# Up-projection by block products: seven products of a pair in another order, and a statistics matmul issued later

## The chip, the cores and the metric

The kernel runs on one core of a Trainium2 chip. The metric is device time in microseconds (us) of one execution, the median of several runs. TensorE (PE) does the matmuls and loads their weights (PEld), VectorE (DVE), ScalarE (ACT) and GpSimd (POOL) the elementwise work, and SyncE (SP) issues the DMAs.

## What is computed

One layer of a hybrid encoder trunk on 512 tokens of width 2048, in float32. The change concerns the feed-forward part alone:

```
h  = h + W_down( relu( RMSNorm(h) W_up )^2 )        W_up: 2048 x 8192, W_down: 8192 x 2048
y  = RMSNorm_final(h)
RMSNorm(x) = x * rsqrt(mean(x*x) + 1e-6) * w
```

Ahead of it stand an input projection, neighbourhood attention, a bidirectional gated delta rule and the output projection, none of which is edited.

## The kernel before

**Operands.** Every float32 matmul operand is split into a high part (a rounding cast on ACT, line 94) and the rest (a subtraction on DVE, line 95); a product is three matmuls, high times high, high times low and low times high (lines 907 to 909). Activations stay transposed: features on partitions, tokens on the free axis.

**Up-projection.** The 8192 output features are taken as 32 pairs of two 128-wide tiles. For one pair, weights and activations are seen as 2 x 2 blocks: A11, A12, A21, A22 are [128, 1024] weight tiles (1024 input features by 128 outputs), and the activations are halved by features and by tokens (lo_t, hi_t, 256 tokens each). As in Strassen's scheme seven products instead of eight are made, each with a sum of weight blocks (S1 = A21 + A22, S2 = S1 + A11, S4 = S2 + A12, S3 = A21 + A11) and a sum of activation blocks (T1 to T4, made once). A product is 8 blocks of 3 matmuls of 256 columns, 24 matmuls. S1, S2 and S4 are made one after the other in place, in the tile of A22 (`p.a22`, later `p.s2`), by adds on DVE (line 914); S3 is made in the tile of A21.

**Banks.** A pair has three PSUM banks, a, b and c (`BANK`, line 920). P6 and P7 add onto what is in bank b (P1, then P1 + P6), P3 onto bank c (P5); Q4, P1, P5 and P2 start a bank anew (`FIRST`). Between two products of one bank, the partial sum is taken out: ACT copies Q4 (line 980), P5 (982), P1 (984) and P6 (986) from PSUM into the halves of two [128, 2, 256] tiles, tA and tB; DVE adds these to the later sums (lines 988 to 995). A matmul into a bank waits for the copy out of it. Then follow a maximum or minimum with zero times the norm's factor (DVE, lines 990 and 999), a square (ACT) and a store to DRAM (SP, lines 1002 and 1003).

**Order.** `ORDER` (line 922) gives the products of a pair: Q4, P5, P1, P6, P7, P3, P2. Pairs 0 and 1 are done together, product by product (line 1050), with P1 and P2 of both made earlier (lines 1013 to 1017); pairs 2 to 29 one at a time; pairs 30 and 31 together (line 1053). The queues of the engines are not filled strictly in the order of the code: at compile time a planner takes, for each engine, the first instruction in code order that its own costs say is ready. In the trace P3 is thus cut in two, with P7 between its parts. On the chip each queue runs in the order so fixed.

**Buffers.** High and low weight parts have three buffers each (line 898), raw weight tiles four, A21/A22 seven (line 1025), tA/tB four (line 1028), and the output tiles r0, r1 share four with the later reloads of hidden tiles (`ev`, line 78).

**Start of the stage.** The last output tiles of the output projection give the sums of squares for the norm (`sumsq`, line 820). `stat` (line 829) is a task that is advanced once every 12 up-projection matmuls (`pump`): at its first step it makes eight matmuls with one column (lines 833 and 834), then DVE's twelve small steps for the reciprocal root and a diagonal tile (lines 142 to 146); three steps later comes the matmul that broadcasts the factor (line 149). Meanwhile ACT and DVE split the activation operands (line 862). The tiles of pairs 0 and 1 lie in memory that the unsplit T1 to T4 (`TR`) held before. After pair 31 the first 16 hidden tiles are reloaded (line 1054) and the down-projection begins.

Of the kernel before, what the change touches and what calls it, by code (L numbers as in the profile page):

```python
# [10 lines left out]
F32 = mybir.dt.float32  # L11
# [8 lines left out]
T = 512  # L20
# [29 lines left out]
def tile_hybrid_block(  # L50
# [5 lines left out]
    V, S_, PE, G = nc.vector, nc.scalar, nc.tensor, nc.gpsimd  # L56
# [20 lines left out]
    def ev(name):  # L77
        return st.tile([128, T], F32, tag="ev", name=name, bufs=4)
# [19 lines left out]
    tasks = []  # L98
# [31 lines left out]
    def rsqrt(pool, a, n, nm):  # L130
        y = pool.tile([128, n], F32, tag="rsy", name=f"rsy_{nm}", bufs=2)
        u = pool.tile([128, n], F32, tag="rsu", name=f"rsu_{nm}", bufs=2)
        return newton_rsqrt(y, u, a)
# [5 lines left out]
    def rstd_bcast(ps, sumsq, nm, cs=range(4), wait=0, dg=None):  # L139
        n, lo = len(cs), cs[0]  # L140
        a = cp.tile([128, 4], F32, tag="rsa", name=f"rsa_{nm}", bufs=2)
        V.tensor_scalar(out=a[:, :n], in0=sumsq[:, lo : lo + n], scalar1=1.0 / D, scalar2=EPS, op0=ALU.mult, op1=ALU.add)
        rs = rsqrt(cp, a[:, :n], n, nm)
        dg = ev(f"dg_{nm}") if dg is None else dg
        V.tensor_tensor(out=dg[:, : n * 128].rearrange("p (c i) -> p c i", c=n), in0=ident[:, None, :].to_broadcast([128, n, 128]),
                        in1=rs[:, :, None].to_broadcast([128, n, 128]), op=ALU.mult)
        for _ in range(wait):
            yield
        PE.matmul(ps[:, lo * 128 : (lo + n) * 128], ones, dg[:, : n * 128], start=True, stop=True)
# [32 lines left out]
    with ExitStack() as p0:  # L182
# [27 lines left out]
        def mtile(key, view=None):  # L210
            ps = mm()
            for u in range(2):
                unit_mm(ps, fetch(key, u), X, 8 * u, u == 0, u == 1, view)
            return ps
# [96 lines left out]
        for r in (127, 0):  # L311
            t = dn.tile([128, 128], F32, name=f"sel{r}")
# [411 lines left out]
        i = 3  # L724
# [40 lines left out]
        for h in range(NH):  # L765
            qkv = []
            for e, kind in enumerate(("aq", "ak", "av")):
                ps = mtile((kind, h), perm)
                t = ap.tile([128, T], F32, tag=kind, name=f"{kind}{h}", bufs=1 if e < 2 else 2)
# [5 lines left out]
            t = att_task(h, *qkv, ap)  # L775
# [8 lines left out]
    with ExitStack() as p1:  # L784
# [3 lines left out]
        def bank():  # L788
            return mmp.tile([128, T], F32, tag="mm", name="ps_b")
# [27 lines left out]
        tp = p1.enter_context(tc.tile_pool(name="tp", bufs=1, side="right", reuse_waits="tile"))  # L817
        acc = tp.tile([128, T], F32, name="sacc")

        def sumsq(src, m, nm, ts=slice(0, T)):  # L820
            sq = tp.tile([128, T], F32, tag="sq", name=f"sq{nm}", bufs=2)
            S_.activation(out=sq[:, ts], in_=src[:, ts], func=AF.Square)
            if m == 0:
                V.tensor_copy(out=acc, in_=sq)
            elif m < 15:
                V.tensor_tensor(out=acc[:, ts], in0=acc[:, ts], in1=sq[:, ts], op=ALU.add)
            return sq

        def stat(nm, sq, cs=range(4)):
            ps = sxp.tile([128, T], F32, tag="sx", name="ps_s")  # L830
            for c in cs:
                b = slice(c * 128, (c + 1) * 128)
                PE.matmul(ps[:, c : c + 1], acc[:, b], ones[:, 0:1], start=True, stop=False)
                PE.matmul(ps[:, c : c + 1], sq[:, b], ones[:, 0:1], start=False, stop=True)
            ps2 = bank()
            yield from rstd_bcast(ps2, ps, nm, cs, 3)
            ts = slice(cs[0] * 128, (cs[-1] + 1) * 128)
            S_.copy(out=rB[:, ts], in_=ps2[:, ts])
            return ps2
# [8 lines left out]
        lo_t, hi_t = slice(0, 256), slice(256, 512)  # L848
# [15 lines left out]
        with ExitStack() as p5:  # L864
# [3 lines left out]
            for n, m in enumerate(m for j in range(8) for m in (j, j + 8)):  # L868
                ps = bank()
# [6 lines left out]
                sq = sumsq(xr, n, f"h{m}")  # L876
# [20 lines left out]
            def wsplit(raw, name):  # L897
                hi = st.tile([128, 1024], F32R, tag="wh", name=f"wh_{name}", bufs=3)
                lo = st.tile([128, 1024], F32R, tag="wl", name=f"wl_{name}", bufs=3)
                return split(raw, hi, lo)  # L900
# [12 lines left out]
            def add(out, x, y, op=ALU.add):  # L913
                V.tensor_tensor(out=out, in0=x, in1=y, op=op)  # L914
# [4 lines left out]
            ROLE = {"P1": "11", "P2": "21", "P3": "22", "Q4": "T4", "P5": "T1", "P6": "T2", "P7": "T3"}  # L919
            BANK = {"P1": "b", "P6": "b", "P7": "b", "P5": "c", "P3": "c", "Q4": "a", "P2": "a"}  # L920
            FIRST = {"P1", "P5", "Q4", "P2"}
            ORDER = ("Q4", "P5", "P1", "P6", "P7", "P3", "P2")

            def open_pair(nm, a11, a12):
                p = Pair()
# [38 lines left out]
            def up_m(i):  # L964
                m0 = i // 8 * 16 + i % 8
                return m0, m0 + 8

            def up_open(i):
                m0, m1 = up_m(i)
                return open_pair(f"u{i}", load_raw(wup[m0, 0], f"A11_u{i}"), load_raw(wup[m0, 1], f"A12_u{i}"))  # L970

            def up_evac(i, p, q, et):
                ps = p.ps[BANK[q]]
                if not hasattr(p, "tA"):
                    p.tA, p.tB = et(f"tA_u{i}"), et(f"tB_u{i}")
                    p.r0, p.r1 = ev(f"r0_u{i}"), ev(f"r1_u{i}")
                    p.left = 7
                tA, tB, r0, r1 = p.tA, p.tB, p.r0, p.r1
                if q == "Q4":
                    S_.copy(out=tA[:, 0], in_=ps)  # L980
                elif q == "P5":
                    S_.copy(out=tB[:, 0], in_=ps)
                elif q == "P1":
                    S_.copy(out=tA[:, 1], in_=ps)  # L984
                elif q == "P6":
                    S_.copy(out=tB[:, 1], in_=ps)
                elif q == "P7":
                    add(r1[:, hi_t], ps, tB[:, 0])
                    add(r1[:, lo_t], ps, tA[:, 0])
                    V.scalar_tensor_tensor(out=r1, in0=r1, scalar=0.0, in1=rB, op0=ALU.min, op1=ALU.mult)  # L990
                    S_.activation(out=r1, in_=r1, func=AF.Square)
                elif q == "P3":
                    add(r0[:, hi_t], ps, tB[:, 1])
                else:
                    add(r0[:, lo_t], ps, tA[:, 1])
                p.left -= 1
                if p.left:
                    return
                V.scalar_tensor_tensor(out=r0, in0=r0, scalar=0.0, in1=rB, op0=ALU.max, op1=ALU.mult)
                S_.activation(out=r0, in_=r0, func=AF.Square)  # L1000
                m0, m1 = up_m(i)
                nc.sync.dma_start(out=hidD[m0], in_=r0)
                nc.sync.dma_start(out=hidD[m1], in_=r1)
# [3 lines left out]
            for i, p in enumerate(first):  # L1007
                for q in ("P1", "P2"):
                    heads[i, q] = wsplit(p.a11 if q == "P1" else p.a12, f"{q}_u{i}") if (i, q) in ((0, "P1"), (0, "P2"), (1, "P1")) else None
            tasks.append(stat("h", sq))  # L1010
            for o, j in early_fill[:8]:
                fill(o, j, tr_src[o, j])
            for i, p in enumerate(first):
# [7 lines left out]
        with ExitStack() as p6:  # L1021
            sm = p6.enter_context(tc.tile_pool(name="sm", bufs=1, side="right", reuse_waits="tile"))

            def a_tile(name):
                return sm.tile([128, 1024], F32, tag="a", name=name, bufs=7)

            def et(name):
                return sm.tile([128, 2, 256], F32, tag="et", name=name, bufs=4)

            def more(p, s22, s21):  # L1030
                p.a22, p.a21 = a_tile(f"A22_{p.nm}"), a_tile(f"A21_{p.nm}")
                nc.sync.dma_start(out=p.a22, in_=s22)
                nc.sync.dma_start(out=p.a21, in_=s21)

            def up_group(idx, order, ps=None):
                ps = ps or [up_open(i) for i in idx]
                for i, p in zip(idx, ps):
                    m0, m1 = up_m(i)
                    more(p, wup[m1, 1], wup[m1, 0])
                if order[0] == "P1":  # L1040
                    for q in ("P1", "P2"):
                        for i, p in zip(idx, ps):
                            up_evac(i, p, q, et)
                    order = order[2:]
                for q in order:
                    for i, p in zip(idx, ps):
                        run_product(p, q, a_tile)
                        up_evac(i, p, q, et)

            up_group((0, 1), ("P1", "P2", "Q4", "P5", "P6", "P7", "P3"), first)  # L1050
            for i in range(2, 30):
                up_group((i,), ORDER)
            up_group((30, 31), ORDER)
            hid0 = [load_hid(k) for k in range(16)]
        p7.close()

# [6 lines left out]
        for b in range(NB):  # L1063
# [4 lines left out]
            for m in range(14 if last else 16):  # L1068
                ps = bank()
# [27 lines left out]
        for half in range(2):  # L1097
            ts = slice(half * 256, half * 256 + 256)
            for m in (14, 15):
                ps = bank()[:, 0:256]  # L1100
# [10 lines left out]
                sq = sumsq(H[m], m, f"f{m}_{half}", ts)  # L1111
# [88 lines left out]
```

## Time and profile before

| | before |
|---|---|
| median of 3 runs (lowest, highest) | 2942.87 us (2940.63, 2944.16) |
| the profiled execution's own time | 2942.32 us |
| its span in the trace | 2940.5 us |
| weight loads busy | 2471.8 us (84%) |
| DVE busy | 1687.3 us (57%) |
| ACT busy | 1032.7 us (35%) |
| POOL busy | 24.7 us (1%) |
| granted TensorE clock, mean | 0.995 |

The profile shows one execution. Busy time is the time in which an engine had an instruction under way; a matmul's end is modelled, and matmuls overlap, so the step from one start to the next tells PE's pace. A wait names the instruction whose end released the waiting one.

### The profile page before, as it was taken

What the parts mean: (1) busy time and instruction counts of PE and PEld (TensorE: products, weight loads), DVE (VectorE), ACT (ScalarE), POOL (GpSimd) and SP (SyncE); (2) the same over time, 40 slices, a digit from 0 to 9 for tenths busy, and PEclk for the clock granted to TensorE, in tenths of its full rate; (3) what the DMA queues carried; (4) which work ended last, traced back from release to release, by engine and by line L of the source; (5) the groups of instructions that cost most, each with busy time, mean ns of one, the idle gap of its engine ahead of it and who ended that gap; (6) DMA issues with size and microseconds to landing.
All of it is one profiled execution on the core that took longest, in us unless ns stands there. A gap on an engine that the chain in (4) does not pass through costs nothing.

```text
span 2940.5 us, 39399 instructions
## 1 busy us (share of the span) xinstructions
PE 2872.9 (98%) x15736; PEld 2471.8 (84%) x15736; DVE 1687.3 (57%) x2495; ACT 1032.7 (35%) x1613; POOL 24.7 (1%) x66
## 2 busy tenths in 40 slices
PE   8999999999999999999999999999999999999998
PEld 6778788888788888888879999999997888888887
DVE  6888779744554444444458777777775242332334
ACT  6444322233233333223345444444444232221322
POOL 0000000000000000000000000000000000000000
PEclk9999999999999999999999999999999999999999
DMA  7555663655632323543434333333428242343332
GB/s 231 191 176 187 212 184 120 213 159 166 187 116 94 95 87 119 170 156 111 145 109 165 126 125 127 119 130 122 129 73 271 94 157 94 114 137 100 108 101 86
DMA packets 170872, 412.30 MB, mean 140 GB/s; under 512 B 34368, under 2 KB 46720, under 8 KB 170688
## 3 DMA queue, kind: packets, MB, share of 16 engines
q1 hardware_dynamic: 170016, 407.69, 43.1%
q0 software_dynamic: 672, 2.10, 0.3%
q8 instruction: 123, 2.02, 0.3%
q14 instruction: 61, 0.50, 0.1%
HBM read 350.84 MB, written 58.88 MB: 139 GB/s over the span
## 4 chain that ended last, share of the span: by engine, by line
PE 88%; DVE 5%; DMA 5%; ACT 1%; issue 1%; SPq 0%; DVEq 0%; ACTq 0%
PE ps_b L115 12%; PE ps_b L116 12%; PE ps_b L117 12%; PE ps_mm L115 9%; PE ps_mm L117 9%; PE ps_mm L116 9%; PE ps_b L907 8%; PE ps_b L909 7%; PE ps_b L908 7%; DVE wl_in L90 1%; DMA bB<-rowD 1%; DMA Nd<-bB 1%; DMA gB<-rowD 1%; DMA kb<-rowD 1%; PE ps_ax L589 0%
## 5 line engine op out<-in xcount | busy, mean ns | idle before, releaser
L115 PE MATMUL ps_mm<-xh,wh_in 128*128 128x512 f32 x1416 | 567.1, 400 | 2.8 <-ACT wh_in L89 2.8
L117 PE MATMUL ps_mm<-xh,wl_in 128*128 128x512 f32 x1416 | 560.1, 396 | 0.5 <-DVE wl_in L90 0.5
L116 PE MATMUL ps_mm<-xl,wh_in 128*128 128x512 f32 x1416 | 559.8, 395 | 0.0
L115 PE MATMUL ps_b<-hih,wh_dn 128*128 128x512 f32 x992 | 386.4, 390 | 2.3 <-ACT hih L94 2.3
L117 PE MATMUL ps_b<-hih,wl_dn 128*128 128x512 f32 x992 | 386.5, 390 | 0.3 <-DVE wl_dn L90 0.3
L116 PE MATMUL ps_b<-hil,wh_dn 128*128 128x512 f32 x992 | 386.5, 390 | 0.2 <-DVE hil L95 0.2
L89 ACT CAST wh_in<-raw_in 128x1024 fp32r<-128x1024 f32 x177 | 186.0, 1051 | 414.6 <-PE ps_mm L116 336.4
L117 PEld LDWEIGHTS ps_mm<-xh,wl_in 128*128 128x128 f32 x1416 | 267.6, 189 | 60.7 <-DVE wl_in L90 1.0
L115 PEld LDWEIGHTS ps_mm<-xh,wh_in 128*128 128x128 f32 x1416 | 267.8, 189 | 58.0 <-ACT wh_in L89 3.2
L116 PEld LDWEIGHTS ps_mm<-xl,wh_in 128*128 128x128 f32 x1416 | 268.0, 189 | 55.1 <-issue 0.2
L89 ACT CAST wh_dn<-raw_dn 128x1024 fp32r<-128x1024 f32 x124 | 130.8, 1055 | 460.4 <-PE ps_b L116 451.0
L90 DVE TENSOR_TENSOR wl_dn<-raw_dn,wh_dn 128x1024 fp32r<-128x1024 f32 x124 | 151.9, 1225 | 232.9 <-ACT wh_dn L89 232.8
L90 DVE TENSOR_TENSOR wl_in<-raw_in,wh_in 128x1024 fp32r<-128x1024 f32 x177 | 216.2, 1222 | 120.2 <-ACT wh_in L89 113.7
L907 PE MATMUL ps_b<-XT_x,wh_S_u 128*128 128x256 f32 x768 | 222.9, 290 | 13.0 <-ACT tA_u L984 12.9
L115 PEld LDWEIGHTS ps_b<-hih,wh_dn 128*128 128x128 f32 x992 | 186.4, 188 | 42.4 <-ACT hih L94 3.9
L116 PEld LDWEIGHTS ps_b<-hil,wh_dn 128*128 128x128 f32 x992 | 186.7, 188 | 40.4 <-DVE hil L95 1.7
L117 PEld LDWEIGHTS ps_b<-hih,wl_dn 128*128 128x128 f32 x992 | 186.7, 188 | 39.2 <-DVE wl_dn L90 0.7
L909 PE MATMUL ps_b<-XT_x,wl_S_u 128*128 128x256 f32 x768 | 217.4, 283 | 0.0
L908 PE MATMUL ps_b<-XT_x,wh_S_u 128*128 128x256 f32 x768 | 217.2, 283 | 0.0
L95 DVE TENSOR_TENSOR wl_S_u<-A_u,wh_S_u 128x1024 fp32r<-128x1024 f32 x128 | 156.2, 1223 | 71.8 <-ACT wh_S_u L94 71.6
L94 ACT CAST wh_S_u<-A_u 128x1024 fp32r<-128x1024 f32 x128 | 134.3, 1049 | 144.8 <-DVE A_u L914 129.6
L907 PEld LDWEIGHTS ps_b<-XT_x,wh_S_u 128*128 128x128 f32 x768 | 147.1, 192 | 23.6 <-ACT tA_u L984 18.7
(354 smaller groups left out, 5101.4 us busy)
## 6 DMA issues: line engine op xcount, KB each, us to landing
raw_in<-in_win SPq DMA_DIRECT2D x177, 512.0 KB
raw_dn<-in_wdn SPq DMA_DIRECT2D x124, 512.0 KB
raw_A_u<-in_wup SPq DMA_DIRECT2D x64, 512.0 KB
A_u<-in_wup SPq DMA_DIRECT2D x64, 512.0 KB
raw_wo<-in_wout SPq DMA_DIRECT2D x32, 512.0 KB
hidD<-r_u SPq DMA_DIRECT2D x64, 256.0 KB
hr<-hidD SPq DMA_DIRECT2D x64, 256.0 KB
gD<-g SPq DMA_DIRECT2D x32, 256.0 KB
```

The source lines that it names most:

```text
L89: S_.copy(out=hi, in_=raw)
L90: V.tensor_tensor(out=lo, in0=raw, in1=hi.bitcast(F32), op=ALU.subtract)
L94: S_.copy(out=hi, in_=src)
L95: V.tensor_tensor(out=lo, in0=src, in1=hi.bitcast(F32), op=ALU.subtract)
L115: PE.matmul(ps, hi[:, w], rh, start=first and kk == 0, stop=False)
L116: PE.matmul(ps, hi[:, w], rl, start=False, stop=False)
L117: PE.matmul(ps, lo[:, w], rh, start=False, stop=last and kk == 7)
L907: PE.matmul(ps, hi[:, c], t[:, lo_t], start=first and j == 0, stop=False, skip_group_check=True)
L908: PE.matmul(ps, hi[:, c], t[:, hi_t], start=False, stop=False, skip_group_check=True)
L909: PE.matmul(ps, lo[:, c], t[:, lo_t], start=False, stop=j == 7, skip_group_check=True)
```

## The change

The products of a pair run in the order Q4, P1, P5, P6, P3, P7, P2, and no two that follow each other write one bank. The copies are regrouped, so that tA holds Q4 and P5, and tB P1 and P6; P7's two adds become one over [128, 2, 256] with its sum read twice. There are six tA/tB buffers instead of four, and one for the squares instead of two. Pairs 30 and 31 are done one after the other. For the norm ahead of the up-projection, the task `stat` lets two steps pass before its matmuls and seven instead of three before the broadcast; for the final norm it stays as it was.

```
         def sumsq(src, m, nm, ts=slice(0, T)):
-            sq = tp.tile([128, T], F32, tag="sq", name=f"sq{nm}", bufs=2)
+            sq = tp.tile([128, T], F32, tag="sq", name=f"sq{nm}", bufs=1)
...
-        def stat(nm, sq, cs=range(4)):
+        def stat(nm, sq, cs=range(4), wait=3, lead=0):
+            for _ in range(lead):
+                yield
             ps = sxp.tile([128, T], F32, tag="sx", name="ps_s")
...
-            yield from rstd_bcast(ps2, ps, nm, cs, 3)
+            yield from rstd_bcast(ps2, ps, nm, cs, wait)
...
-            ORDER = ("Q4", "P5", "P1", "P6", "P7", "P3", "P2")
+            ORDER = ("Q4", "P1", "P5", "P6", "P3", "P7", "P2")
...
                 elif q == "P5":
+                    S_.copy(out=tA[:, 1], in_=ps)
+                elif q == "P1":
                     S_.copy(out=tB[:, 0], in_=ps)
-                elif q == "P1":
-                    S_.copy(out=tA[:, 1], in_=ps)
...
                 elif q == "P7":
-                    add(r1[:, hi_t], ps, tB[:, 0])
-                    add(r1[:, lo_t], ps, tA[:, 0])
+                    add(r1.rearrange("p (o t) -> p o t", o=2), ps[:, None, :].to_broadcast([128, 2, 256]), tA)
...
                 else:
-                    add(r0[:, lo_t], ps, tA[:, 1])
+                    add(r0[:, lo_t], ps, tB[:, 0])
...
-            tasks.append(stat("h", sq))
+            tasks.append(stat("h", sq, wait=7, lead=2))
...
             def et(name):
-                return sm.tile([128, 2, 256], F32, tag="et", name=name, bufs=4)
+                return sm.tile([128, 2, 256], F32, tag="et", name=name, bufs=6)
...
-            for i in range(2, 30):
+            for i in range(2, 32):
                 up_group((i,), ORDER)
-            up_group((30, 31), ORDER)
```

## Rows read from the trace of the kernel before

**Rows 1.** The page, busy time and share of the span of each engine.
```profile
PE 2872.9 (98%) x15736; PEld 2471.8 (84%) x15736; DVE 1687.3 (57%) x2495; ACT 1032.7 (35%) x1613; POOL 24.7 (1%) x66
```

**Rows 2.** Stages: length, busy time (instructions) of PE, PEld, DVE, ACT, POOL, PEclk, DMA.
```profile
1530.50:1552.30 21.80, 16.30 (x116) 14.63 (x115) 18.91 (x56) 15.86 (x42) 0.00 (x0) 0.92 0.27 88
...
1583.00:2177.80 594.80, 581.39 (x4706) 567.93 (x4705) 437.59 (x477) 269.31 (x365) 0.00 (x0) 1.00 0.37 122
2177.80:2218.00 40.20, 40.20 (x338) 40.20 (x337) 31.63 (x35) 19.95 (x28) 0.00 (x0) 1.00 0.30 97
2218.00:2245.00 27.00, 24.19 (x92) 17.23 (x91) 14.82 (x22) 12.80 (x20) 0.00 (x0) 0.94 0.87 287
```

**Rows 3.** Waits from 1583 to 2177 us: who for whom, us, times, longest.
```profile
PEld ps_b L907 <- ACT tA_u L984: 18.7, 28, 0.7
...
PE ps_b L907 <- ACT tA_u L984: 12.9, 28, 0.5
PEld ps_b L907 <- ACT tB_u L986: 4.9, 28, 0.2
PEld ps_b L909 <- DVE wl_S_u L95: 3.3, 14, 0.2
```

**Rows 4.** Timeline of one pair, 1803.7 to 1809.6: start, us, instruction, idle before.
```profile
1803.92 0.28 PE L909 MATMUL ps_b<-X_x,wl_A_u 128*128 128x256 f32 x1
...
1804.24 0.37 ACT L984 COPY tA_u<-ps_b 128x256 f32<-128x256 f32 x1 [1.25 <-PE ps_b L909]
...
1804.66 0.39 PE L907 MATMUL ps_b<-XT_x,wh_S_u 128*128 128x256 f32 x1 [0.46 <-ACT tA_u L984]
1804.88 0.28 PE L908 MATMUL ps_b<-XT_x,wh_S_u 128*128 128x256 f32 x1
...
1808.72 0.36 ACT L986 COPY tB_u<-ps_b 128x256 f32<-128x256 f32 x1
...
1808.88 0.28 PE L908 MATMUL ps_b<-X_x,wh_S_u 128*128 128x256 f32 x1
1809.13 0.39 PE L907 MATMUL ps_b<-XT_x,wh_S_u 128*128 128x256 f32 x1
```

**Rows 5.** Groups by line and shape: busy us, mean ns, idle before.
```profile
L95 DVE TENSOR_TENSOR wl_S_u<-A_u,wh_S_u 128x1024 fp32r<-128x1024 f32 x128 | 156.2, 1223 | 71.8 <-ACT wh_S_u L94 71.6
L94 ACT CAST wh_S_u<-A_u 128x1024 fp32r<-128x1024 f32 x128 | 134.3, 1049 | 144.8 <-DVE A_u L914 129.6 <-PE ps_b L908 12.0 <-issue 3.2
L914 DVE TENSOR_TENSOR A_u<-A_u,raw_A_u 128x1024 f32<-128x1024 f32 x96 | 116.8, 1220 | 1.0
L1072 DVE TENSOR_TENSOR Ha<-ps_b,Ha 128x512 f32<-128x512 f32 x62 | 42.9, 692 | 187.6 <-PE ps_b L117 187.6
```

**Rows 6.** The chain that ended last, 1532 to 1558: start, us, what.
```profile
1532.62 0.22 PE ps_s L833 x2
...
1535.29 1.06 ACT wh_P_u L94
...
1548.18 2.44 DVE XT_x L95 x7
...
1550.65 0.65 ACT tA_u L984 x2
...
1552.27 1.24 DVE wl_A_u L95
```

**Rows 7.** Timeline, 1533 to 1544: the root's first and last steps, the broadcast.
```profile
1533.99 0.16 DVE L142 TENSOR_SCALAR rsa_h<-ps_s 128x4 f32<-128x4 f32 x1 [1.15 <-PE ps_s L834]
...
1536.18 0.16 DVE L127 SCALAR_TENSOR_TENSOR rsy_h<-rsu_h,rsy_h 128x4 f32<-128x4 f32 x1
...
1542.62 2.08 PE L149 MATMUL ps_b<-dg_h,ones 128*128 128x512 f32 x2 [4.13 <-DVE dg_h L145]
```

**Rows 8.** The chain that ended last, 2205 to 2226: start, us, what.
```profile
2218.85 4.01 DMA hr<-hidD
...
2223.55 0.74 PE ps_b L115 x2
```

## The prediction

> **What bounds the kernel now.** The page first: TensorE (PE) is busy 98% of the 2940.5 us span [rows 1], so time can only come off where PE is slowed or kept waiting. The table by stage shows where that is. The up-projection's single pairs, from the first product of pair 2 to the first of pair 30, take 594.8 us for 28 pairs of 168 matmuls (4704; the row counts 4706, as two belong to the edges): 21.24 us a pair, 126.4 ns a matmul. The last two pairs, whose products alternate, take 40.2 us for 336: 20.1 us a pair, 119.6 ns a matmul. The granted clock is 1.00 (2.4 GHz) in both, and the matmuls are alike [rows 2]. So a pair run alone costs 1.14 us more than the same work with two pairs interleaved.
>
> The view of waits for this stretch says why: PE and its weight load wait 28 times, once a pair, for the ACT copy of L984 (P1's copy), and the weight load 28 times for that of L986 (P6's copy) [rows 3]. One pair in the timeline shows both. P1's last matmul starts at 1803.92; its copy runs 1804.24 to 1804.61; P6, which adds into the same bank, starts at 1804.66, and its second matmul at 1804.88. Two steps that at 0.12 us each take 0.24 us took 0.96: 0.72 us lost. P6's copy starts only at 1808.72, and P7, again the same bank, at 1809.13, 0.25 us after the last matmul of P3 that the planner had put in between; some 0.25 us is lost there [rows 4]. That makes 0.97 of the 1.14; the rest is the split-up P3, half of whose weights come late in every second pair (the weight load's 14 waits) [rows 3].
>
> How much is there to win? By PE's busy time the stage has 13.4 us of idle, by the weight load's busy time 26.9, by the spacing 594.8 - 28 x 20.1 = 32.0 [rows 2]. The Trainium skill (Perfetto Trace Analysis, section Identifying the Most-Contended Engine) calls matmul busy time a poor measure, since matmuls are pipelined, and prefers the weight load's share: by it the gain would be about 27 us. The trace agrees with the order of the two; I take the spacing, because a delayed pair of matmuls also counts longer (0.39 us at 1804.66 [rows 4]).
>
> **The change, part by part.** *New order Q4, P1, P5, P6, P3, P7, P2.* Between P1 and P6 now lies P5 (bank c), between P6 and P7 lies P3, between P5 and P3 lies P6: each copy has a whole product, 24 x 0.1196 = 2.87 us. The copy needs 0.37 us and started 0.32 us after the last matmul where ACT was free [rows 4]; behind one 1.05 us cast [rows 5] it ends after some 1.7 us. Both waits go. What is late next? The weights: S1, S2 and S4 are made in place in one tile, and P5, P6, P3 now follow each other. Take Q4's start as 0. S1's cast needs a weight buffer (three rotate) that the previous pair's P2 frees at 0; with 1.05 for a cast, 1.22 for a subtraction or an add [rows 5]: S1 ready at 2.3 (wanted at 5.7), S2 added, cast and subtracted by 5.8 (wanted at 8.6), S4 by 9.3 (wanted at 11.5). Slack 2.2 us at the tightest. DVE is busy 437.59 of 594.8 us [rows 2], so one foreign 1.22 us step per link is fine, two are just over. I take no new stall: 28 x 1.14 = **-32.0 us**. Ends: all of it, or up to half kept (below).
>
> *One evacuation add of 512 elements for two of 256, tA/tB regrouped:* 0.69 us (same size out of PSUM) to 1.22 us (1024 elements) [rows 5]; by size the first. The next product writes another bank, so only the squaring behind it waits: 0. Its store goes out one product later in the pair, and what SP has queued behind it with it; those loads are for later pairs: 0. *Six tA/tB buffers:* no wait for them in the pairs' view [rows 3]: 0. *One squares buffer:* each square now waits for the previous add into the running sum, one output tile ago: 0; uncovered, one add, 0.69 us.
>
> *Last two pairs one after the other:* alternating they ran without stall; in the new order also: 0. But pair 30 now ends 20 us before pair 31, so its two output buffers are free for the first reloads of the hidden tiles. Now the third reload leaves at 2218.85 and PE has the tile 4.7 us later [rows 8]; the stretch has 27 us with clock 0.94 [rows 2]. The slot it takes is freed by the split of the first, and with that tile already there the split can follow P2's first blocks, by an estimate up to half a product (1.4 us) sooner: **-1.0**. Ends: -3 (PE's idle 27.0 - 24.2 us [rows 2]) and +2 (pair 31's own stores now both come last).
>
> *Statistics matmuls two steps later, broadcast seven steps after instead of three.* PE visibly stands 4.13 us before the broadcast, as the diagonal tile comes late from DVE [rows 7]. But the chain that ended last does not pass there: it goes from P1's end (cast at 1535.29) over DVE's splits of the transformed operands to 1550.62, ACT's copies, and the split of A22 at 1552.27 [rows 6]. PE would wait there instead, so the visible stall is worth 0. The eight statistics matmuls, on the chain at 0.22 us each, leave it: up to 1.8 us; in return DVE's twelve small root steps, from 1533.99 to 1536.34, now done in idle time (2.4 us), may fall into its busy run [rows 6, 7]. The larger tA/tB pool moves those tiles, whose copies wait for the operands' last reader at 1550.65 [rows 6]. Net **-0.5**; ends -4.1 (the whole stall) and +2.1 (both broadcast passes, 2.08 us, on PE's path [rows 7]).
>
> Sum: -32.0 - 1.0 - 0.5 = -33.5. I keep back 1.5 us for pairs at the edges (pair 2 follows the group in the old order): -32. The profiled execution took 2942.32 us (1.8 around the span), 0.55 below the median of 2942.87. 2942.3 - 32 = 2910.3; on the median's scale **2911 us**.
>
> **The rivals.** *A quarter to half of the stall stays:* DVE runs two foreign steps inside the chain S1, S2, S4, so P3 starts late by 2.44 - 2.2 = 0.24 us, or three, 1.46 us, in some pairs. At 0.24 to 0.5 us a pair 7 to 14 us are given back: 2918 to 2925. For it: three dependent products in a row, DVE at 74%. Against: the operations of P3 are issued ahead of those of P7.
>
> *Slower:* S3's subtraction stands before S4's add in DVE's queue. It waits for its cast, whose buffer P5 frees at 8.6: cast to 9.7, subtraction to 10.9, then S4's add, cast, subtraction to 14.4, against 11.5 wanted: 2.9 us a pair, +81 us, so about 2992. It turns the sign when P3 comes over 1.14 us late in each pair. For it: in the old order S3 did go first on DVE. Against: the order by which the planner prefers steps has changed with the products.
>
> *No change:* the copy is not what PE waits for but a buffer that the copy frees, and the order only moves the bubble: 2943. The Trainium skill (the same page and section) reads a gap that repeats through a stretch as a sign of too little SBUF or PSUM for the next tile; by that this order would give nothing. Against it: the matmul after the gap adds into a bank already held, and it starts 0.05 us after the copy's end [rows 4].
>
> *The visible 4.1 us at the start go as well:* about 2907; inside the range.
>
> **How the numbers follow.** Forecast with its bounds (2903 to 2916): 0.76. Part of the stall kept (2916 to 2936): 0.16. No change: 0.04. Slower: 0.04. The lower bound is -32 - 4.1 - 3 = 2903.8, the upper takes in half of the second case: 2903 to 2921. A measurement of this kernel tells 0.2%, 5.9 us, from nothing. Faster 0.92, same 0.04, slower 0.04.
>
> **What would show it.** Right: no waits of PE for tB or tA copies in the pairs; a pair takes 20.1 us; PE's weight-load share of this stage near 1.00; P3 in one piece. At the start, PE's wait moves from the broadcast to Q4's first weights, and the first product of pair 2 starts within 2 us of 1583. Wrong: PE waiting once a pair for S2's or S4's weights (wl from DVE), or a pair still at 21 us.

## The result, and the profile after

The changed kernel takes 2910.45 us (median of four, 2907.69 to 2918.87) beside 2942.32 us of the kernel before (2940.63 to 2944.16): a ratio of 0.9896, with a 95% interval of 0.9875 to 0.9918. (The kernel before has a fourth run here, and so a median 0.55 us below that of the three runs above.) The forecast was 2911, within 2903 to 2921. The profiled execution of the changed kernel is its slowest, 2918.87 us with a span of 2917.1; that has to be kept apart first, and a table by stage does it (from starts of TensorE's products, us):

| | before | after | difference |
|---|---|---|---|
| to the first product of pair 0 | 1530.56 | 1538.06 | +7.5 |
| head: to pair 2's first product | 52.42 | 51.91 | -0.5 |
| pairs 2 to 29 | 594.86 | 563.54 | -31.3 |
| pairs 30 and 31 | 40.25 | 40.25 | 0 |
| from the end of pair 31's last product to the end of the span | 722.4 | 723.3 | +0.9 |

The first line holds one edit alone, the single buffer for the squares (they are made in the output projection, so that stage is not quite unedited), and that shows no cost: over the 14 profiles of this study the line lies between 1526.4 and 1538.1 us with one buffer and between 1530.6 and 1534.1 us with two. The 7.5 us are the scatter of single executions, and the stages below are what can be compared to a microsecond.

The page's first row of the changed kernel, which answers to [rows 1]:

```profile
PE 2858.2 (98%) x15736; PEld 2471.7 (85%) x15736; DVE 1686.6 (58%) x2463; ACT 1036.1 (36%) x1613; POOL 24.7 (1%) x66
```

Shares hardly move, because 31 us come off 2940. The table by stage of the changed kernel (columns as in [rows 2]) tells more:

```profile
1590.00:2153.40 563.40, 563.40 (x4706) 563.40 (x4705) 438.85 (x449) 271.31 (x364) 0.00 (x0) 1.00 0.39 129
2153.40:2193.70 40.30, 40.30 (x339) 40.30 (x337) 30.64 (x32) 20.01 (x27) 0.00 (x0) 1.00 0.30 96
2193.70:2220.70 27.00, 22.19 (x87) 16.85 (x87) 15.50 (x22) 13.96 (x21) 0.00 (x0) 0.94 0.88 286
```

The same 4706 matmuls take 563.4 us in place of 594.8, and now both PE and its weight load are busy for the whole of it. The view of waits for PE and for the weight load is empty in this stretch; the four lines of [rows 3] have no successor. A pair takes 20.13 us, as each of the last two did before the change, and P3's 24 matmuls follow each other in one piece. DVE has 28 instructions fewer, the joined add, whose group (by line and shape) reads:

```profile
L916 DVE TENSOR_TENSOR r_u<-ps_b,tA_u 128x512 f32<-128x512 f32 x28 | 19.2, 684 | 0.0
```

At the head, the long wait has moved, as the timeline of PE shows, from the broadcast (4.13 us in [rows 7], now 1.75) to Q4's first weights (4.25):

```profile
1553.23 1.12 PE L149 MATMUL ps_b<-dg_h,ones 128*128 128x512 f32 x2 [1.75 <-DVE dg_h L145]
1558.61 0.58 PE L909 MATMUL ps_b<-XT_x,wh_A_u 128*128 128x256 f32 x1 [4.25 <-ACT wh_A_u L94]
```

### The profile page after: what moved, and what is told of

The parts are those of the page before. It is cut to its first block, busy times and chain, and to the rows that moved or that the text cites. A ratio compares the mean times of both kernels' runs of the same rounds, so it can differ in the third digit from the quotient of the medians.

```text
span 2917.1 us, 39363 instructions
## 1 busy us (share of the span) xinstructions
PE 2858.2 (98%) x15736; PEld 2471.7 (85%) x15736; DVE 1686.6 (58%) x2463; ACT 1036.1 (36%) x1613; POOL 24.7 (1%) x66
## 4 chain that ended last, share of the span: by engine, by line
PE 87%; DMA 6%; DVE 5%; ACT 1%; issue 1%; SPq 0%; DVEq 0%; ACTq 0%
PE ps_b L116 12%; PE ps_b L115 12%; PE ps_b L117 12%; PE ps_mm L116 8%; PE ps_mm L115 8%; PE ps_mm L117 8%; PE ps_b L911 7%; PE ps_b L909 7%; PE ps_b L910 7%; DMA bB<-rowD 1%; DMA Nd<-bB 1%; DVE wl_in L90 1%; DMA raw_x<-in_x 1%; DMA XQ<-Nd 1%; DMA kb<-rowD 1%
## 5 line engine op out<-in xcount | busy, mean ns | idle before, releaser
L1072 DVE TENSOR_TENSOR Ha<-ps_b,Ha 128x512 f32<-128x512 f32 x62 | 42.9, 692 | 189.3 <-PE ps_b L117 189.3
```

Source lines behind the costliest of these rows:

```text
L1072: V.tensor_tensor(out=H[m], in0=ps, in1=H[m], op=ALU.add)
```

## The experiments

**1. The order alone.** The kernel before, with nothing but the new list:

```
-            ORDER = ("Q4", "P5", "P1", "P6", "P7", "P3", "P2")
+            ORDER = ("Q4", "P1", "P5", "P6", "P3", "P7", "P2")
```

> The kernel before with the new order of products alone: the old grouping of the copies, two adds behind P7, four tA/tB buffers, two buffers for squares, the statistics where they were, pairs 30 and 31 together. Theory (the gain is the waits on the copies of P1 and P6): a pair from 2 to 29 takes 20.1 us instead of 21.24, PE waits for no copy there, and the time is 2911 us (2909 to 2914). Rival (the other edits are needed, above all the six tA/tB buffers or the one add): a pair stays above 20.5 us and the time above 2920 us.

Measured: 2913.76 us, ratio 0.9892 (0.987 to 0.9913). The head is 52.43 us with its 4.1 us wait before the broadcast, as before; the pairs run in 563.5 us. Its window over pairs 2 to 29:

```profile
1586.60:2150.00 563.40, 563.40 (x4705) 563.40 (x4705) 443.25 (x477) 271.35 (x364) 0.00 (x0) 1.00 0.39 129
```

The order gives the whole gain; the other edits together, regrouped copies, the joined add (477 DVE instructions here, 449 in the full change) and six tA/tB buffers among them, give nothing that can be measured.

**2. The statistics alone.** The kernel before, with the later statistics matmuls and broadcast:

```
-            tasks.append(stat("h", sq))
+            tasks.append(stat("h", sq, wait=7, lead=2))
```

> The kernel before with the later statistics matmuls and the later broadcast alone. Theory (the 4.1 us at the start are not on the chain; DVE's splits of the operands are): PE's wait before the broadcast shrinks and that before Q4's first weights grows by as much; from the first product to pair 2 the kernel before takes 52.4 us, this one 51 to 54; the time is 2942 us, within 2 us. Rival (the visible wait is time): 48 us, and 2938 us in all.

Measured: 2939.66 us, ratio 0.9992 (0.9979 to 1.0004): no change that can be told, though 0.3 us under the expected stretch. Head 52.75 us, pairs 594.87. PE's waits in the head:

```profile
PE ps_b L909 <- ACT wh_A_u L94: 4.5, 1, 4.5
PE ps_b L149 <- DVE dg_h L145: 1.8, 1, 1.8
```

The long wait stands before Q4 instead of before the broadcast, and moving it is worth nothing; the rival's head of 48 us did not come. Q4 does start 0.9 us earlier (20.81 us after the first product, 21.73 before), but that is lost again behind it, as the part on the statistics below shows.

**3. The old order without the two copies.** P1's and P6's ACT copies are left out from pair 2 on, all buffers and `ORDER` staying as before. This kernel does not compute that part of the up-projection: the sums that used the two copies read Q4's and P5's instead.

```
                 elif q == "P1":
-                    S_.copy(out=tA[:, 1], in_=ps)
+                    if i < 2:
+                        S_.copy(out=tA[:, 1], in_=ps)
...
```

> The kernel before in its old order, without the ACT copies of P1 and P6 in pairs 2 to 31 (the sums that used them read Q4's and P5's copies instead, so this part of the up-projection is not computed). Theory (what PE waits for is the copy): the pairs take 20.1 to 20.3 us in the old order too, time 2911 to 2915 us. Rival (a buffer shortage or late weights of S2 and S3): still about 21 us a pair and 2940 us.

Measured: 2911.23 us (one run); head 52.42, and pairs 2 to 29:

```profile
1584.10:2147.60 563.50, 563.50 (x4706) 563.50 (x4705) 440.14 (x478) 256.86 (x309) 0.00 (x0) 1.00 0.40 129
```

Without the copies the old order is as fast as the new one: the stall came from the copy of the bank just filled, and not from a shortage of buffers. The planner, with no copy to bridge, also left P3 in one piece behind P7, and with that the waits for P3's late weights are gone too.

**4. Another order without neighbours.** `ORDER` Q4, P5, P1, P2, P6, P3, P7 in the changed kernel.

> The changed kernel with another order in which no two neighbours share a bank: Q4, P5, P1, P2, P6, P3, P7. Theory (any such order does it): 20.1 to 20.3 us a pair, 2908 to 2914 us. Rival (the particular order matters, through the weights S1, S2, S4): over 20.6 us a pair, 2923 us or more.

Measured: 2912.14 us (one run), pairs 2 to 29 in 563.55 us. Both orders tried in which no two products of one bank follow each other run without a wait in the pairs.

**5. One seam put back: P6 and P7.** In the changed kernel:

```
-            ORDER = ("Q4", "P1", "P5", "P6", "P3", "P7", "P2")
+            ORDER = ("Q4", "P1", "P5", "P6", "P7", "P3", "P2")
```

> The changed kernel with the order Q4, P1, P5, P6, P7, P3, P2: of the products for one bank P6 and P7 follow each other, all others have another bank between. Theory (the stall is TensorE waiting for the copy of the bank it has just filled, so each pair of neighbours costs one wait): P7 waits for ScalarE's copy of P6; with some of P3 taken ahead 0.2 to 0.4 us a pair, 6 to 12 us over the 30 pairs, so 2917 to 2922; with nothing taken ahead 0.7 us or more a pair, about 2932. Rival (the gain comes from the earlier Q4 and P5 alone): no cost, about 2910.

Measured: 2925.57 us (one run), 20.75 us a pair, 0.62 more, 18.7 us in all: between the two expected values. The wait is not where it was expected. PE's timeline at the end of P6:

```profile
1736.05 0.28 PE L911 MATMUL ps_b<-XT_x,wl_S_u 128*128 128x256 f32 x1
1736.17 0.28 PE L909 MATMUL ps_b<-X_x,wh_S_u 128*128 128x256 f32 x1
1736.29 0.28 PE L910 MATMUL ps_b<-X_x,wh_S_u 128*128 128x256 f32 x1
1737.26 0.39 PE L911 MATMUL ps_b<-X_x,wl_S_u 128*128 128x256 f32 x1 [0.70 <-DVE wl_S_u L95]
```

X_x with wh_S is P3: the planner has put its first matmuls into the gap that it saw for the copy. PE takes its queue in order, so when P3's third matmul wants the low part of S4, which is late, PE stands, and P7 with it; P6's copy, too, runs only from 1737.24, behind a cast on ACT. A wait of 0.7 us comes in every second pair, 15 times; in the pairs between, the same matmul starts some 0.2 us late.

**6. The other seam: P1 and P6.** `ORDER` Q4, P5, P1, P6, P3, P7, P2 in the changed kernel.

> The changed kernel with the order Q4, P5, P1, P6, P3, P7, P2: only P1 and P6 follow each other in one bank, and P3 parts P6 from P7. With the run that made P6 and P7 neighbours this splits the gain of 1.12 us a pair into its two seams. By the prediction's reading of the timeline (two matmuls that take 0.96 in place of 0.24 us): 0.72 us a pair, 30 pairs, +21.6 us, about 2932. By subtraction of what the neighbours P6 and P7 cost (0.63 us a pair measured): 0.49 us a pair, +15 us, about 2925. Rival (the wait at one seam only shows when the other is there too): less than 0.2 us a pair, below 2916.

Measured: 2938.8 us, ratio to the kernel before 0.9987 (0.9974 to 1.0); 21.06 us a pair, 0.93 more, over both expected values. PE's timeline at the end of P1, and under it ACT's:

```profile
1734.34 0.28 PE L911 MATMUL ps_b<-X_x,wl_A_u 128*128 128x256 f32 x1
1735.25 0.39 PE L909 MATMUL ps_b<-X_x,wh_S_u 128*128 128x256 f32 x1 [0.63 <-ACT wh_S_u L94]
1735.47 0.28 PE L910 MATMUL ps_b<-X_x,wh_S_u 128*128 128x256 f32 x1
1735.59 0.32 PE L909 MATMUL ps_b<-XT_x,wh_S_u 128*128 128x256 f32 x1
```

```profile
1734.15 1.05 ACT L94 CAST wh_S_u<-A_u 128x1024 fp32r<-128x1024 f32 x1 [1.97 <-DVE A_u L916]
1735.10 0.37 ACT L986 COPY tB_u<-ps_b 128x256 f32<-128x256 f32 x1
```

Again two matmuls of P3 lie ahead of P6 in the queue. The wait that the profile names is the one for their cast (1734.15), which went ahead of P1's copy on ACT; the copy, which in [rows 4] starts 0.32 us after the last matmul, here started 0.76 after it and ended at 1735.47, and P6 starts 0.12 us later. So in neither of the two orders does PE wait for the copy itself by the label: what is measured is the seam together with what the planner puts into it. One seam alone costs 0.62 or 0.93, but both together 1.12 (31.3 / 28): they don't add up. The queues differ from order to order (P3's piece in the seam is 2 matmuls here, 6 or 11 in experiment 5, 9 or 11 in the kernel before), which we take for the reason.

**7. How much slack the chain of weights has.** Four more adds of 512 columns on DVE in every pair from the third, into a tile that nobody reads any more:

```
                     w = wsplit(s2, f"S2_{nm}")
...
+                    if int(nm[1:]) >= 2:
+                        for e in range(4):
+                            add(acc, p.s2[:, :T], p.s2[:, T:])
```

> The changed kernel with four more additions of 512 columns on VectorE (0.61 us each by the row of its like, 2.4 us together) between the splitting of S2 and the additions for S4 in every pair from the third: how much slack the chain of weights has ahead of P3. By the slack worked out by hand ahead of the change (2.2 us): 0.2 us a pair, about 6 us, 2916. By the slack that the trace of the changed kernel shows between the end of S4's subtraction and P3 (1.1 us): 1.3 us a pair, about 39 us, 2949. Rival (VectorE has room for all of it): no cost, 2910.

Measured: 2938.21 us (one run), 20.88 us a pair, 0.76 more, 22.7 us over the 30 pairs: between the two values that were expected. First the timeline of the changed kernel itself, DVE and then PE at P3's start:

```profile
1740.24 2.45 DVE L95 TENSOR_TENSOR wl_S_u<-A_u,wh_S_u 128x1024 fp32r<-128x1024 f32 x2 [1.17 <-ACT wh_S_u L94]
```

```profile
1742.34 0.28 PE L909 MATMUL ps_b<-X_x,wh_S_u 128*128 128x256 f32 x1
...
1742.58 0.28 PE L911 MATMUL ps_b<-X_x,wl_S_u 128*128 128x256 f32 x1
```

The row of 1740.24 holds two subtractions, S4's first, ready at 1741.47; P3's third matmul, the first to read it, starts at 1742.58. Slack 1.11 us. With the four adds (two rows of two), DVE and PE:

```profile
1737.88 1.42 DVE L916 TENSOR_TENSOR sacc<-A_u 128x512 f32<-128x512 f32 x2
...
1740.35 1.41 DVE L916 TENSOR_TENSOR sacc<-A_u 128x512 f32<-128x512 f32 x2
...
1744.19 2.36 DVE L95 TENSOR_TENSOR wl_S_u<-A_u,wh_S_u 128x1024 fp32r<-128x1024 f32 x2 [1.17 <-ACT wh_S_u L94]
```

```profile
1744.64 0.28 PE L910 MATMUL ps_b<-X_x,wh_S_u 128*128 128x256 f32 x1
1745.42 0.39 PE L909 MATMUL ps_b<-XT_x,wh_S_u 128*128 128x256 f32 x1 [0.50 <-ACT tB_u L991]
1745.65 0.28 PE L911 MATMUL ps_b<-X_x,wl_S_u 128*128 128x256 f32 x1
```

S4's low part is ready at about 1745.4, 12.4 us after its pair's Q4 (1733.04) in place of 10.6 (1741.47 - 1730.86): of the added work, four steps of 0.7 us, 1.8 us reach it; the rest goes into DVE's wait for S2's cast. 1.8 - 1.1 = 0.7 us late, about what a pair loses. The label shows another thing: PE waits for P6's copy, because the planner, seeing S4 late, put one matmul of P7 ahead. At this place both come at 1745.4, so which of the two costs the time can't be told.

**8. The end grouped as before.** Pairs 30 and 31 together again in the changed kernel:

```
-            for i in range(2, 32):
+            for i in range(2, 30):
                 up_group((i,), ORDER)
+            up_group((30, 31), ORDER)
```

> The changed kernel with its last two pairs grouped as in the kernel before. Theory (the grouping of the end moves only a few microseconds at the transition to the down-projection): within 1.5 us of the changed kernel, so 2909 to 2912, and from the first matmul of the down-projection to the end 722.4 us as before the change in place of 723.3. Rival (the edit at the end gives part of the gain): 3 us or more slower.

Measured: 2907.07 us (one run), 2 us under the expected stretch and within the spread of the changed kernel's own runs (2904.13 to 2918.87 in eight); 722.1 us from the end of the pairs on. The grouping of the end is worth nothing that shows.

**9. The reloads on another queue.** In the changed kernel:

```
-            nc.sync.dma_start(out=raw, in_=hidD[k])
+            (nc.gpsimd if k < 16 else nc.sync).dma_start(out=raw, in_=hidD[k])
```

> The changed kernel with the first 16 reloads of the hidden activations for the down-projection issued from GpSimd's DMA queue in place of SP's. Theory (the reloads' buffers are free early, but SP issues them in order behind the loads of the down-projection's weights, which wait for their buffers): the reloads leave earlier and the time from the first matmul of the down-projection to the end shrinks by 1 to 4 us from 723.3, so 2906 to 2910. Rival (the reloads wait for what they reload, not for the queue): no change, 2910.

Measured: 2916.57 us (one run), and from the end of the pairs on 731.2 us, 8 longer than in the changed kernel: the theory failed. The queue did hold the reloads back. On SP, in the changed kernel:

```profile
2178.23 12.52 SPq L82 DMA_DIRECT2D raw_dn<-in_wdn  x3
2190.85 0.85 SPq L845 DMA_DIRECT2D hr<-hidD  x2
...
2196.43 2.69 SPq L845 DMA_DIRECT2D hr<-hidD  x4
```

and on GpSimd in the experiment:

```profile
2170.15 0.56 POOL L845 DMA_DIRECT2D hr<-hidD  x1 [1.82 <-ACT tB_u L986]
2185.11 1.09 POOL L845 DMA_DIRECT2D hr<-hidD  x2 [14.40 <-DVE hil L95]
```

The second now leaves 13 us before the pairs end (2183.6); in the changed kernel the first two leave 3 us before it. But the third still waits for the split of the first, and SP, rid of the reloads, issues sixteen 256 KB loads of the residual (L1061) between 2184 and 2196. The window after the pairs, the reloads in its chain of waits, and last the longest reload in that chain of the changed kernel:

```profile
2183.60:2210.60 27.00, 18.00 (x61) 11.88 (x60) 11.92 (x16) 10.90 (x16) 7.08 (x13) 0.91 0.97 349
```

```profile
2185.11 2.89 DMA hr<-hidD
...
2191.97 5.97 DMA hr<-hidD
...
2199.60 7.12 DMA hr<-hidD
```

```profile
2197.48 4.88 DMA hr<-hidD
```

DMA is at 0.97 (0.88 in the changed kernel), a reload of the chain takes up to 7.1 us in place of at most 4.9, and PE does 61 matmuls in place of 87. Our reading is that SP's order had kept the residual's loads out of the reloads' way; that these loads are the cause, and not the queue itself, was not tried alone.

**10. A quarter of the T operands' low parts on GpSimd.** In the changed kernel:

```
+            if o[0] == "T" and j % 3 == 2:
+                S_.copy(out=t[:, lo_t], in_=src)
+                G.tensor_tensor(out=t[:, hi_t], in0=src, in1=t[:, lo_t].bitcast(F32), op=ALU.subtract)
+                return
```

> The changed kernel with 8 of the 32 subtractions that give the low parts of the T operands on GpSimd in place of VectorE. Theory (VectorE's run of fills ahead of the second pair's weights bounds the head of the up-projection): 8 times 0.34 us leave VectorE, and the head from the first product to the third pair shrinks from 51.9 to about 49.3 us, so 2907 to 2909. Rival (the weights' DMA or ScalarE's chain bounds the head): head unchanged at 51.9, 2910.

Measured: 2914.54 us (one run), head 55.48 us in place of 51.9 to 52.6: the opposite. GpSimd's subtractions, and DVE's at the same time:

```profile
1537.44 1.71 POOL L866 TENSOR_TENSOR XT_x<-TRT,XT_x 128x256 fp32r<-128x256 f32 x2 [422.26 <-ACT XT_x L865]
1539.89 1.69 POOL L866 TENSOR_TENSOR XT_x<-TRT,XT_x 128x256 fp32r<-128x256 f32 x2 [0.74 <-ACT XT_x L865]
```

```profile
1537.25 0.42 DVE L892 SCALAR_TENSOR_TENSOR TRT<-TRT,xr 128x256 f32<-128x256 f32 x1
1538.47 3.73 DVE L95 TENSOR_TENSOR XT_x<-TRT,XT_x 128x256 fp32r<-128x256 f32 x6
1542.53 0.70 DVE L122 TENSOR_SCALAR rsu_h<-rsa_h 128x4 int32<-128x4 int32 x1
```

Six subtractions take 3.73 us, a step of 0.62 each, where the step is 0.34 undisturbed, and an instruction of four columns takes 0.70 in place of 0.15. The diagonal tile is ready to be made 18.1 us after the first product in place of 14.4, and the broadcast is late by that. The Trainium skill (SBUF — State Buffer, section SBUF: two separate sides) says that GpSimd and DVE share a pair of ports, which a DVE instruction with two inputs in SBUF (as these subtractions have) and a GpSimd one that reads SBUF hold in turn, each for the whole instruction, while the other stands. The trace agrees: the subtraction that starts 0.12 us after one of GpSimd's takes 0.96 us, one with none beside it 0.41. Whether DVE's fills bound the head remains open, as this edit slowed them.

**11. Both edits of 9 and 10, and the changed kernel again on the same chip.**

> The changed kernel with both edits: the first 16 reloads on GpSimd's DMA queue, and 8 low-part subtractions on GpSimd. If both theories hold the gains add up: 3 to 6 us below the changed kernel, 2904 to 2907. If neither does: 2910.

> The changed kernel itself again, on the same chip as the kernel with both edits, so that a difference of a few microseconds can be read: 2907 to 2914.

Measured: 2924.88 us with both (ratio to before 0.9932, 0.9916 to 0.9948), 2910.48 without (0.9881, 0.9865 to 0.9897). Neither expected value came: the two edits together are 14 us slower than none, and in the profile the head takes 54.1 us and the end 731.5. No version measurably beat the changed kernel.

## Why the prediction was right

**The pairs (-32.0).** Right in mechanism, place and size: -31.3 on the chip. The small excess is the 20.1 us taken for a pair where it is 20.13. The order alone (1), the old order without the copies (3) and another order (4) all end at 563.5 us, so the copy between two products of one bank is shown to be the cause. The spacing was the right measure. The weight load's share, which the Trainium skill prefers to matmul busy time (Perfetto Trace Analysis, section Identifying the Most-Contended Engine), gave 27. The Trainium skill's other remark, that a gap repeating through a stretch can mean too little room for the next tile (the same page, but section Optimization Strategy, not the one that the prediction names), does not fit this gap: in 3 it went without a buffer added.

**Its breakdown holds for the old queue, and not as prices.** The prediction put 0.72 us on P1 and P6, 0.25 on P6 and P7, 0.17 on P3's late weights. Summing the late starts of PE over the 28 pairs of the kernel before gives 0.72, 0.23 and 0.15 us a pair. But one seam alone costs 0.62 or 0.93 (5, 6): each part stands where the planner had left it after filling gaps with P3, and can't be carried to another order, as the expectation of 6 did.

**The weights' chain (slack 2.2 us).** The step "S4 by 9.3 (wanted at 11.5)" was mis-sized: ready at 10.6, wanted at 11.7, slack 1.1 us (7). DVE's steps for the previous pair stand in it: S1's subtraction starts 0.4 us after its cast, and S2's add stands behind one of 0.6 us. It changed nothing here, but the rival of a stall partly kept was nearer than thought. The slower rival did not come: S4's subtraction stands ahead of S3's on DVE.

**The joined add (0.69).** Measured 0.68, hidden as forecast; and no wait for the larger pool.

**The last two pairs (0) and the transition (-1.0).** The pairs: 40.25 us, right. The transition failed: +0.9 in this profile, 722.4 in the repeated one, against 722.4 before. The step that failed is "its two output buffers are free for the first reloads": the reloads stood on SP behind three loads of down-projection weights until 2190.85, 2.9 us ahead of the end of the pairs, where before the change the first two left 5.8 us ahead of it:

```profile
2212.33 0.86 SPq L843 DMA_DIRECT2D hr<-hidD  x2
```

The third left 2.7 us after the last product, not 0.8 [rows 8], and PE's first matmul of the down-projection, before the change right behind the last product, came 1.7 us after it. That the buffers were free by then is borne out by experiment 9, where the first two reloads leave 16 and 13 us ahead; what leaving early is worth by itself it can't tell, as the residual's loads moved too.

**The statistics (-0.5).** Measured -0.5 in this profile, which is luck: the sum lacked a term. Its own two terms came. DVE's run of steps starts 1.8 us earlier, without the statistics matmuls ahead of it, and the twelve root steps inside it cost 0.07 us each, 0.9 in all where up to 2.4 was feared. So Q4 starts 20.55 us after the first product in place of 21.73, 1.2 earlier; then the head loses 0.7. The clock column of a table by windows shows why. Columns as in [rows 2]; the clock is the third from the right. Before the change, from the broadcast on and from Q4 on:

```profile
1542.60:1546.00 3.40, 3.38 (x10) 2.35 (x11) 3.40 (x11) 3.40 (x12) 0.00 (x0) 0.54 0.00 0
...
1552.20:1557.40 5.20, 3.83 (x27) 3.42 (x28) 5.06 (x5) 2.51 (x4) 0.00 (x0) 1.00 0.97 396
```

After it, from the broadcast on and from Q4 on:

```profile
1553.20:1558.60 5.40, 1.12 (x2) 0.30 (x2) 4.78 (x15) 2.23 (x5) 0.00 (x0) 0.79 0.55 178
1558.60:1563.20 4.60, 4.13 (x17) 3.83 (x18) 4.53 (x4) 2.10 (x2) 0.00 (x0) 0.50 1.02 415
```

Both kernels have a stretch at about the lower level (1.2 GHz; 0.54 and 0.50 in the rows) after PE's wait of over 4 us. Before, it fell on the broadcast and the end of the P products, off the chain of [rows 6], and Q4 ran at 1.00; now it falls on Q4, where a matmul steps by 0.21 us in place of 0.12:

```profile
1560.46 0.41 PE L910 MATMUL ps_b<-XT_x,wh_A_u 128*128 128x256 f32 x1
1560.67 0.41 PE L911 MATMUL ps_b<-XT_x,wl_A_u 128*128 128x256 f32 x1
```

The sign "within 2 us of 1583" for pair 2's first product failed by the letter in this execution (1589.97), as 7.5 us went by ahead of pair 0; in the repeated one it held (1583.33).

**The 1.5 us held back** for the edges were not needed; they made up for the transition's missing 1.0 and part of the pairs' 0.7. By the stages behind the first line the change is worth -30.9 us in this profile and -31.1 in the repeated one, by the medians -31.9. That the total came within a microsecond of 2911 is luck as far as the last microsecond goes: the stages ahead of pair 0 alone scatter by more than that from one execution to the next.

## What to carry to other kernels

Where a matmul adds into a bank whose content another engine must first take out, put a product for another bank between the two; here that was worth 1.12 us a pair, with no work saved. Compare orders as wholes: a planner that fills gaps replans every one, so the cost of a seam can't be read off one order and taken to another. A queue that holds a transfer back may be keeping another one out of its way, and where a long stall is moved, the stretch at a low clock that followed it here moved along.

## What was not expected of the hardware

The stretch at about 1.2 GHz after Q4's start differs between executions with this head: its matmuls step by 0.21 us until 4.0 to 6.1 us after Q4's start in the changed kernel and its variants of 4 to 9, and the head goes with it, from 51.62 (4.0 us) to 52.64 (6.1 us), 52.1 on the mean of eight profiles. With the old head three profiles gave 52.42, 52.43 and 52.42. So the later broadcast made the head uneven: at its shortest 0.8 us better, at its longest 0.2 worse, and 0.3 better on the mean. And an instruction of four columns on DVE, 0.15 us, took 0.70 beside a GpSimd instruction.
